# Right-stack tiles at multiples of 128 bytes, and attention's sums over the keys as 512-column products

## The chip, the cores and the metric

The kernel runs on one core of a Trainium2 chip. The metric is the time of one execution on the device in microseconds; three runs of the kernel before gave 663.28 (median), 661.22 and 663.50.

## The reference

One layer of an encoder: a residual stream of 512 positions by 2048 features goes through RMS norm and one input projection, then through two head groups side by side, and one output projection adds it back.

```python
h = rms_norm(x, norm_w)
proj = jnp.einsum('bsd,de->bse', h, w_in)
q, k, v, g_attn, xr, g_lru = jnp.split(proj, SPLITS, axis=-1)
attn_out = attention_group(q, k, v, q_norm_w, k_norm_w)   # 8 heads of 128, 2 key/value heads
lru_out = lru_group(xr, conv_w, conv_b, ...)              # two linear recurrences over 1024 channels
mixed = jnp.concatenate([rms_norm(attn_out, attn_norm_w) * jax.nn.silu(g_attn),
                         rms_norm(lru_out, lru_norm_w) * jax.nn.silu(g_lru)], axis=-1)
return x + jnp.einsum('bse,ed->bsd', mixed, w_out)
```

Attention is full (512 queries by 512 keys, no mask): `s = q k^T * scale`, `p = softmax(s)`, `o = p v`, all in float32. The change concerns the last of the three, the sum over the keys, and where tiles lie in the core's memory (SBUF).

## The kernel before, in words

**Precision.** Each float32 operand of a large product is split into a high and a low part. `mm3` (lines 143 to 147) then makes three products into one accumulator: high x high (line 145), high x low of the moving side (146) and low of the stationary side x high (147). In a row of the profile `mm<-kt,b` the tile named first is the moving operand and the second the stationary one (the weights that are loaded).

**Stages.** The input projection runs in column blocks of 512. First the two blocks of the recurrence's input (`proj_feat`; stationary `wh`/`wl`, moving the turned input `x`), with the recurrence of each half woven into the next block; then keys, values and queries (`proj_tok`; here `x` is stationary and `wh`/`wl` move); then three blocks of gates (`gates`, `proj_feat` again) with attention woven in; a last block of gates; and then the output projection, 672 products on line 890, whose weights `w_out` are combined and split (`oh`, `ol`, lines 704 and 705) as they are needed.

**Attention.** It goes through 8 heads of 4 tiles of 128 queries, step by step (`attention`). In step i: `weights` makes the scores of tile i (3 products of 512 keys, moving `kt`), takes the row maximum on DVE (line 563), the exponential and its sum on ACT (566), the reciprocal on DVE (567), and multiplies by it on POOL (568). `turn_weights` turns tile i-2 with four transposes (575), casts it into the high part on ACT (577) and makes the low part on DVE (578). `values` then sums over the keys for a half head, two tiles: 4 x 3 products with `v` stationary and the turned weights moving, 256 columns wide, whenever the second tile of a half is ready. The sum goes to SBUF by a copy on DVE (590); once per head its square goes through ACT (596) and POOL (597) into a running sum. After each step come two steps of the gate projection, 12 products (`yield STEPS`). DMA issues that prepare sums of `w_out` in memory outside the core are woven into POOL's work (735, 738).

**What sets the order.** On TensorE, and in attention on POOL, the order is that in which the code issues the work (`manual_schedule`); DVE and ACT are ordered by a scheduler in attention and by hand in the output stage. SyncE issues the loads.

**Memory.** Pools are opened on two stacks, left and right, that grow towards each other. The right one starts with a small tile, `end`, of 8 float32 numbers per partition. In the built program every larger tile under it, but for attention's nine `k2`, starts 64 bytes off a multiple of 128; those nine lie under small columns (`sm`, `mx`) and start at a multiple. On the left, the input `x`, the weights `wh`/`wl` of pool `xw`, and the last of the output's operands start at multiples of 128. On the right lie the recurrence's tiles (pool `lru`), `kt`, `v`, the queries and turned weights (`b`, from the ring `b4`), part of the output's operands (pool `fin`, `hq`), and, from the values' split to the end of the query projection, a second pool of `wh`/`wl` named `wx`: `wsplit` (line 196 on) takes the two pools in turn. PSUM, which receives the products, has four buffers for projections (`pj`) and four for the rest (`mm`).

Of the kernel before, what the change touches and what calls it, by code (L numbers as in the profile page):

```python
# [10 lines left out]
F32 = mybir.dt.float32  # L11
F32R = mybir.dt.float32r
AF = mybir.ActivationFunctionType
# [3 lines left out]
P = 128  # L17
SEQ = 512
DM = 2048
KT = DM // P  # L20
NT = SEQ // P
# [9 lines left out]


LRU_K2, LRU_B4 = 12, 9
ATT_K2, ATT_B4 = 9, 9


AHEAD = 600
# [18 lines left out]
def hybrid_kernel(  # L56
# [20 lines left out]
    nc = tc.nc  # L77
# [4 lines left out]
    pools, order = {}, {"left": [], "right": []}  # L82

    def opened(name, side):
        pools[name] = tc.alloc_tile_pool(name=name, bufs=1, side=side, reuse_waits="tile")
        order[side].append(name)
        return pools[name]
# [8 lines left out]
    cp = opened("cp", "left")  # L96
    opened("wr", "left")
    opened("xw", "left")
    opened("end", "right").tile([P, 8], F32, tag="end", name="end")
    hring = opened("hq", "right").ring(8 * 2048, name="hring")  # L100
    aring = pools["hq"].ring(8 * 2048, name="aring")
    opened("lru", "right")
# [5 lines left out]
    def nm(s):  # L108
        cnt[0] += 1
        return f"{s}_{cnt[0]}"  # L110
# [4 lines left out]
    def work():  # L115
        return ("lru", LRU_K2, LRU_B4) if "lru" in pools else ("att", ATT_K2, ATT_B4)

    def k2(dt=F32, shape=(P, SEQ)):
        pool, n, _ = work()
        return pools[pool].tile(list(shape), dt, tag="k2", bufs=n, name=nm("k2"))  # L120

    def b4(dt=F32, shape=(P, 2, SEQ)):
        pool, _, n = work()
        return pools[pool].tile(list(shape), dt, tag="b4", bufs=n, name=nm("b4"))
# [10 lines left out]
    def mm():  # L135
        return ps.tile([P, SEQ], F32, tag="mm", name=nm("mm"))
# [4 lines left out]
    def f(ap):  # L141
        return ap.bitcast(F32)

    def mm3(acc, lh, ll, rh, rl, start, stop):
        nc.tensor.matmul(acc, lh, rh, start=start, stop=False)  # L145
        nc.tensor.matmul(acc, lh, rl, start=False, stop=False)  # L146
        nc.tensor.matmul(acc, ll, rh, start=False, stop=stop)  # L147
# [371 lines left out]
    def turn(rot, h):  # L519

        pt = mm()
        for t in range(NT):
            nc.tensor.transpose(pt[:, t * P : (t + 1) * P], rot[t][:, h, :], ident)  # L523
        return pt

    def split_ps(pt, hi, lo):
        nc.scalar.copy(hi, pt)
        nc.vector.tensor_sub(lo, pt, f(hi))
# [21 lines left out]
    def turned(rot, h):  # L550

        q = b4(F32R)
        split_ps(turn(rot, h), q[:, 0, :], q[:, 1, :])
        return q[:, 0, :], q[:, 1, :]

    def weights(q, g, t):

        qh, ql = q
        tt = slice(t * P, (t + 1) * P)
        sc = mm()  # L560
        mm3(sc, qh[:, tt], ql[:, tt], kth[g], ktl[g], True, True)
        mx = pools["att"].tile([P, 1], F32, tag="mx", bufs=6, name=nm("mx"))
        nc.vector.tensor_reduce(mx, sc, axis=AX.X, op=ALU.max, negate=True)  # L563
        p = k2()
        sm = pools["att"].tile([P, 1], F32, tag="sm", bufs=6, name=nm("sm"))
        nc.scalar.activation(p, sc, AF.Exp, bias=mx, accum_out=sm)
        nc.vector.reciprocal(sm, sm)
        nc.gpsimd.tensor_scalar(p, p, sm, 0.0, op0=ALU.mult, op1=ALU.add)
        return p

    def turn_weights(p, t, pth, ptl):
        tt = slice(t % 2 * P, (t % 2 + 1) * P)
        pt = mm()
        for s in range(NT):
            nc.tensor.transpose(pt[:, s * P : (s + 1) * P], p[:, s * P : (s + 1) * P], ident)  # L575
        p3 = pt.rearrange("p (s q) -> p s q", q=P)
        nc.scalar.copy(pth[:, :, tt], p3)  # L577
        nc.vector.tensor_sub(ptl[:, :, tt], p3, f(pth[:, :, tt]))

    def values(h, half, pth, ptl):  # L580

        gs = slice(h // G * HD, (h // G + 1) * HD)
        o = mm()[:, : 2 * P]
        for s in range(NT):
            mm3(o, vh[s][:, gs], vl[s][:, gs], pth[:, s, :], ptl[:, s, :], s == 0, s == NT - 1)
        if half == 0 and h % 2 == 0:
            ap_[h // 2] = aring.tile([P, 2, SEQ], F32, name=nm("av"))
        av, asum = ap_[h // 2][:, h % 2, :], sums["a"]
        to = slice(half * 2 * P, (half + 1) * 2 * P)
        nc.vector.tensor_copy(av[:, to], o)  # L590
        if half == 1:
            if h == 0:
                nc.scalar.activation(asum, av, AF.Square)
            else:
                sq = k2()
                nc.scalar.activation(sq, av, AF.Square)
                nc.gpsimd.tensor_add(asum, asum, sq)

    def attention(rots):

        qs, ps_, pts = {h: turned(rots[0], h) for h in range(2)}, {}, {}
        yield 13
        last = NH * NT
        for i in range(last + 3):
            h, t = divmod(i, NT)
            if i < last:
                ps_[i] = weights(qs[h], h // G, t)
                if t == 0 and h + 2 < NH:
                    qs[h + 2] = turned(rots[(h + 2) // G], (h + 2) % G)
            j = i - 2  # L610
            if 0 <= j < last:
                h, t = divmod(j, NT)
                if t % 2 == 0:
                    pts[j // 2] = b4(F32R, (P, NT, 2 * P)), b4(F32R, (P, NT, 2 * P))
                turn_weights(ps_.pop(j), t, *pts[j // 2])
            j = i - 3
            if j >= 0 and j % 2 == 1:
                values(j // NT, j // 2 % 2, *pts.pop(j // 2))
            yield STEPS


# [410 lines left out]
    with tc.manual_schedule(engines={mybir.EngineType.Pool}):  # L1032
        weave(fill, attention(rots))
        for _ in range(6):
            next(fill)
# [106 lines left out]
```

## Time and profile before

| | |
|---|---|
| runs | 663.28 us median of 3 (661.22 to 663.50) |
| profiled execution | 663.34 us, of which the span from first to last instruction is 661.5 |
| instructions | 8826 |
| TensorE products | 3067 records |
| attention with the gates | about 280 to 436 us of the span |
| output projection | about 502 to 661 us |

In the rows, PE is TensorE's products, PEld its weight loads, DVE is VectorE, ACT ScalarE, POOL GpSimd, SP SyncE. A product's duration is longer than the distance to the next product's start, since products overlap: a product of 512 columns has a duration of about 390 ns in the rows, and the next starts some 230 ns after it. So distances of starts are read, not durations. "Idle before" is the time in which an engine stood still ahead of a group, with what released it.

### The profile page before, as it was taken

The numbers are of one execution on the slowest core, as the hardware profiler recorded it, in microseconds if no ns is written. First come the engines' busy times: TensorE is split into PE (matmuls) and PEld (weight loads), VectorE is DVE, ScalarE is ACT, GpSimd is POOL, SyncE is SP. The second block draws the span as 40 slices with busy tenths as digits, with TensorE's granted clock in tenths as the row PEclk, the third lists the DMA queues.
The fourth block names the chain that finished last, engine by engine and source line by source line (L and its number), as shares of the span: only waits on it lengthen the run. The fifth ranks groups of instructions, "written<-read, shape, count | busy, mean of one in ns | idle before, by whom it ended". The sixth has DMA issues, their size and how long they took to land.

```text
span 661.5 us, 8826 instructions
## 1 busy us (share of the span) xinstructions
PE 654.1 (99%) x3067; PEld 540.6 (82%) x3067; DVE 490.6 (74%) x851; ACT 346.0 (52%) x639; POOL 91.8 (14%) x121
## 2 busy tenths in 40 slices
PE   8999999999999999999999999999999999999997
PEld 6888888888888888888888888888888878888875
DVE  4879688977687952855865569528967998698994
ACT  3543799489856514454644437435444564333441
POOL 0000000000012301223253335410000000010000
PEclk9999999999999999999999999999999999999999
DMA  8843252322334221345776768762355766585322
GB/s 289 272 143 96 65 141 90 97 64 64 83 106 151 81 90 32 97 138 149 152 168 164 216 128 180 176 153 79 89 164 207 264 215 216 211 290 192 125 83 95
DMA packets 52732, 96.19 MB, mean 145 GB/s; under 512 B 4184, under 2 KB 14544, under 8 KB 52560
## 3 DMA queue, kind: packets, MB, share of 16 engines
q1 hardware_dynamic: 45648, 75.17, 36.0%
q0 software_dynamic: 6720, 19.93, 13.1%
q10 hardware_dynamic: 320, 0.53, 0.3%
q8 instruction: 24, 0.39, 0.2%
q14 instruction: 20, 0.16, 0.1%
HBM read 91.42 MB, written 20.97 MB: 170 GB/s over the span
## 4 chain that ended last, share of the span: by engine, by line
PE 88%; DVE 4%; issue 3%; DMA 3%; POOL 1%; ACT 0%; DVEq 0%; ACTq 0%; POOLq 0%
PE pj L145 19%; PE pj L147 19%; PE pj L146 19%; PE mm L890 9%; PE pj L890 7%; PE mm L146 3%; PE mm L147 3%; PE mm L145 3%; DVE ol L705 2%; PE mm L575 2%; DMA rw<-ts 2%; PE mm L230 1%; PE pj L287 1%; PE mm L523 1%; DMA nw_st<-in_norm_w_dram 1%
## 5 line engine op out<-in xcount | busy, mean ns | idle before, releaser
L145 PE MATMUL pj<-x,wh 128*128 128x512 f32 x376 | 150.2, 400 | 0.0
L147 PE MATMUL pj<-x,wl 128*128 128x512 f32 x376 | 147.1, 391 | 0.0
L146 PE MATMUL pj<-x,wh 128*128 128x512 f32 x376 | 146.7, 390 | 0.0
L204 ACT CAST wh<-wr 128x512 fp32r<-128x512 f32 x144 | 86.5, 617 | 75.9 <-PE pj L147 29.0
L205 DVE TENSOR_TENSOR wl<-wr,wh 128x512 fp32r<-128x512 f32 x144 | 99.5, 711 | 30.7 <-ACT wh L204 30.5
L147 PEld LDWEIGHTS pj<-x,wl 128*128 128x128 f32 x376 | 70.6, 188 | 15.4
L146 PEld LDWEIGHTS pj<-x,wh 128*128 128x128 f32 x376 | 70.8, 188 | 14.0 <-issue 0.5
L145 PEld LDWEIGHTS pj<-x,wh 128*128 128x128 f32 x376 | 70.7, 188 | 13.8 <-issue 0.5
L145 PE MATMUL pj<-wh,x 128*128 128x512 f32 x192 | 75.7, 394 | 0.0
L146 PE MATMUL pj<-wl,x 128*128 128x512 f32 x192 | 75.3, 392 | 0.0
L147 PE MATMUL pj<-wh,x 128*128 128x512 f32 x192 | 75.2, 392 | 0.0
L704 ACT CAST oh<-rw 128x512 fp32r<-128x512 f32 x94 | 54.8, 619 | 31.8 <-PE mm L890 14.5
L705 DVE TENSOR_TENSOR ol<-rw,oh 128x512 fp32r<-128x512 f32 x94 | 60.6, 686 | 9.2 <-ACT oh L704 6.8
L890 PE MATMUL mm<-ol,mh 128*128 128x512 f32 x128 | 50.2, 392 | 0.5 <-DVE ol L705 0.5
L890 PE MATMUL mm<-oh,mh 128*128 128x512 f32 x128 | 50.3, 393 | 0.0
L890 PE MATMUL mm<-oh,ml 128*128 128x512 f32 x128 | 50.2, 392 | 0.0
L577 ACT CAST b<-mm 128x512 fp32r<-128x512 f32 x32 | 18.7, 585 | 58.7 <-PE mm L575 58.7
L563 DVE TENSOR_REDUCE mx<-mm 128x1 f32<-128x512 f32 x32 | 22.0, 688 | 31.2 <-PE mm L147 30.9
L145 PEld LDWEIGHTS pj<-wh,x 128*128 128x128 f32 x192 | 36.1, 188 | 8.1 <-issue 0.2
L146 PEld LDWEIGHTS pj<-wl,x 128*128 128x128 f32 x192 | 36.1, 188 | 8.1 <-issue 0.2
L147 PEld LDWEIGHTS pj<-wh,x 128*128 128x128 f32 x192 | 36.1, 188 | 7.9
L890 PE MATMUL pj<-oh,mh 128*128 128x512 f32 x96 | 37.8, 394 | 0.0
(207 smaller groups left out, 1153.7 us busy)
## 6 DMA issues: line engine op xcount, KB each, us to landing
wr<-in_w_in_dram SPq DMA_DIRECT2D x71, 512.0 KB, 3.7
rw<-in_w_out_dram SPq DMA_DIRECT2D x63, 256.0 KB, 3.9
ts<-in_w_out_dram POOLq DMA_DIRECT2D x24, 512.0 KB, 6.9
rw<-ts SPq DMA_DIRECT2D x31, 256.0 KB, 5.0
ts<-ts POOLq DMA_DIRECT2D x8, 512.0 KB, 5.7
xt<-in_x_dram SPq DMA_DIRECT2D x8, 512.0 KB, 8.2
b<-in_x_dram SPq DMA_DIRECT2D x7, 512.0 KB, 7.7
out_dram<-xt POOLq DMA_DIRECT2D x12, 256.0 KB, 3.0
```

The costliest lines, as they stand in the source:

```text
L145: nc.tensor.matmul(acc, lh, rh, start=start, stop=False)
L146: nc.tensor.matmul(acc, lh, rl, start=False, stop=False)
L147: nc.tensor.matmul(acc, ll, rh, start=False, stop=stop)
L204: nc.scalar.copy(hi, raw[:, k, :])
L205: nc.vector.tensor_sub(lo, raw[:, k, :], f(hi))
L230: nc.tensor.transpose(pt[:, t * P : (t + 1) * P], xc[:, t, ks], ident)
L563: nc.vector.tensor_reduce(mx, sc, axis=AX.X, op=ALU.max, negate=True)
L575: nc.tensor.transpose(pt[:, s * P : (s + 1) * P], p[:, s * P : (s + 1) * P], ident)
L577: nc.scalar.copy(pth[:, :, tt], p3)
L704: nc.scalar.copy(hi, src)
L705: nc.vector.tensor_sub(lo, src, f(hi))
L890: nc.tensor.matmul(bank[name, s], lh[:, a, ts_], rh, start=i == 0 and j == 0, stop=i == 7 and j == 2,)
```

## The change

1. `end` becomes 24 numbers wide (96 bytes instead of 32). In the built program all right-stack tiles then start at a multiple of 128 bytes; attention's `k2` tiles now start 64 off. Nothing else is done to them.
2. The turned weights of a whole head go into one pair of tiles (`pt`, 128 x 4 x 512, high and low), which has two buffers, so one pair. They came from the ring `b4`, a pair per half head; the ring keeps four buffers for the queries.
3. `values` runs once per head: 12 products of 512 columns instead of twice 12 of 256, and one copy of 512 columns.
4. In a step, `values` now stands ahead of `turn_weights`, so that the pair has been read before the next head's first tile is written into it.

```diff
--- before.py
+++ after.py
@@ -31,7 +31,7 @@
 
 
 LRU_K2, LRU_B4 = 12, 9
-ATT_K2, ATT_B4 = 9, 9
+ATT_K2, ATT_B4, ATT_PT = 9, 4, 2
 
 
 AHEAD = 600
@@ -96,7 +96,7 @@
     cp = opened("cp", "left")
     opened("wr", "left")
     opened("xw", "left")
-    opened("end", "right").tile([P, 8], F32, tag="end", name="end")
+    opened("end", "right").tile([P, 24], F32, tag="end", name="end")
     hring = opened("hq", "right").ring(8 * 2048, name="hring")
     aring = pools["hq"].ring(8 * 2048, name="aring")
     opened("lru", "right")
@@ -569,7 +569,7 @@
         return p
 
     def turn_weights(p, t, pth, ptl):
-        tt = slice(t % 2 * P, (t % 2 + 1) * P)
+        tt = slice(t * P, (t + 1) * P)
         pt = mm()
         for s in range(NT):
             nc.tensor.transpose(pt[:, s * P : (s + 1) * P], p[:, s * P : (s + 1) * P], ident)
@@ -577,24 +577,22 @@
         nc.scalar.copy(pth[:, :, tt], p3)
         nc.vector.tensor_sub(ptl[:, :, tt], p3, f(pth[:, :, tt]))
 
-    def values(h, half, pth, ptl):
+    def values(h, pth, ptl):
 
         gs = slice(h // G * HD, (h // G + 1) * HD)
-        o = mm()[:, : 2 * P]
+        o = mm()
         for s in range(NT):
             mm3(o, vh[s][:, gs], vl[s][:, gs], pth[:, s, :], ptl[:, s, :], s == 0, s == NT - 1)
-        if half == 0 and h % 2 == 0:
+        if h % 2 == 0:
             ap_[h // 2] = aring.tile([P, 2, SEQ], F32, name=nm("av"))
         av, asum = ap_[h // 2][:, h % 2, :], sums["a"]
-        to = slice(half * 2 * P, (half + 1) * 2 * P)
-        nc.vector.tensor_copy(av[:, to], o)
-        if half == 1:
-            if h == 0:
-                nc.scalar.activation(asum, av, AF.Square)
-            else:
-                sq = k2()
-                nc.scalar.activation(sq, av, AF.Square)
-                nc.gpsimd.tensor_add(asum, asum, sq)
+        nc.vector.tensor_copy(av, o)
+        if h == 0:
+            nc.scalar.activation(asum, av, AF.Square)
+        else:
+            sq = k2()
+            nc.scalar.activation(sq, av, AF.Square)
+            nc.gpsimd.tensor_add(asum, asum, sq)
 
     def attention(rots):
 
@@ -607,15 +605,18 @@
                 ps_[i] = weights(qs[h], h // G, t)
                 if t == 0 and h + 2 < NH:
                     qs[h + 2] = turned(rots[(h + 2) // G], (h + 2) % G)
+            j = i - 3
+            if j >= 0 and j % NT == NT - 1:
+                values(j // NT, *pts.pop(j // NT))
             j = i - 2
             if 0 <= j < last:
                 h, t = divmod(j, NT)
-                if t % 2 == 0:
-                    pts[j // 2] = b4(F32R, (P, NT, 2 * P)), b4(F32R, (P, NT, 2 * P))
-                turn_weights(ps_.pop(j), t, *pts[j // 2])
-            j = i - 3
-            if j >= 0 and j % 2 == 1:
-                values(j // NT, j // 2 % 2, *pts.pop(j // 2))
+                if t == 0:
+                    pts[h] = [
+                        pools["att"].tile([P, NT, SEQ], F32R, tag="pt", bufs=ATT_PT, name=nm("pt"))
+                        for _ in range(2)
+                    ]
+                turn_weights(ps_.pop(j), t, *pts[h])
             yield STEPS
```

TensorE's order at the first head's sums, before. Here `k` is a tile of softmax weights, `b` a half head's turned weights (high and low), `v` the values, `pj` a gate projection:

```order
L523 MATMUL mm_2802<-ident,ev_2043 128x128
L575 MATMUL mm_2811<-ident,k_551_2721 128x128 x4
L145 MATMUL mm_2818<-b_553_2726,v_1912 128x256
L146 MATMUL mm_2818<-b_554_2727,v_1912 128x256
L147 MATMUL mm_2818<-b_553_2726,v_1912 128x256
```

After nine more such rows the projection goes on. With the change (the end of the scores, the first sums):

```order
L145 MATMUL mm_2871<-kt_2207,b_508_2519 128x512
L146 MATMUL mm_2871<-kt_2207,b_508_2519 128x512
L147 MATMUL mm_2871<-kt_2207,b_508_2519 128x512
L145 MATMUL mm_2882<-pt_2726,v_1912 128x512
L146 MATMUL mm_2882<-pt_2727,v_1912 128x512
L147 MATMUL mm_2882<-pt_2726,v_1912 128x512
```

and behind nine more of these:

```order
L145 MATMUL mm_2882<-pt_2726,v_1921 128x512
L146 MATMUL mm_2882<-pt_2727,v_1921 128x512
L147 MATMUL mm_2882<-pt_2726,v_1921 128x512
L575 MATMUL mm_2900<-ident,k_568_2796 128x128 x4
L145 MATMUL pj_2528<-x_87_440,wh_2855 128x512
```

The sums moved from behind the transposes to between the scores and the transposes, and two steps later, to where the head's fourth tile is there; the transposes are followed by the projection.

DVE at the same place (`mx` maximum, `sm` reciprocal, `av` the copy of the sums; line numbers of the change are one lower at the copy), before:

```order
L578 TENSOR_TENSOR b_573_2810<-mm_2811,b_572_2809 128x4x128
L590 COPY av_2831<-mm_2818 128x256
L563 TENSOR_REDUCE mx_2850<-mm_2846 128x1
L578 TENSOR_TENSOR b_573_2810<-mm_2857,b_572_2809 128x4x128
L205 TENSOR_TENSOR wl_2963<-wr_2960,wh_2962 128x512
```

and with the change:

```order
L578 TENSOR_TENSOR pt_2727<-mm_2840,pt_2726 128x4x128
L205 TENSOR_TENSOR wl_2947<-wr_2944,wh_2946 128x512
L567 RECIPROCAL sm_2836<-sm_2836 128x1
L205 TENSOR_TENSOR wl_2951<-wr_2944,wh_2950 128x512
L563 TENSOR_REDUCE mx_2875<-mm_2871 128x1
L567 RECIPROCAL sm_2878<-sm_2878 128x1
L589 COPY av_2895<-mm_2882 128x512
L578 TENSOR_TENSOR pt_2899<-mm_2900,pt_2898 128x4x128
```

The copy comes once per head, behind the next step's maximum and reciprocal, and the next head's first split stands right behind it. On POOL and SyncE the order is the same as before.

## The prediction

> **What bounds the kernel now.** I read the page first: shares of busy time, then the chain that ended last.
>
> ```profile
> span 661.5 us, 8826 instructions
> PE 654.1 (99%) x3067; PEld 540.6 (82%) x3067; DVE 490.6 (74%) x851; ACT 346.0 (52%) x639; POOL 91.8 (14%) x121
> PEclk9999999999999999999999999999999999999999
> PE 88%; DVE 4%; issue 3%; DMA 3%; POOL 1%; ACT 0%; DVEq 0%; ACTq 0%; POOLq 0%
> ```
>
> TensorE is busy 654.1 of 661.5 us at full clock, and is 88% of the chain. What is left to gain lies inside its stream: the distance from the start of one product to the start of the next, which busy time doesn't show because products overlap. So the second reading is of starts. Where a stretch holds nothing but 512-column products, the first and the last start of one line, with its count, give three products per step (one for each line of `mm3`). Columns: shortest/median/longest duration in ns, first and last start in us.
>
> ```profile
> L147 PE MATMUL pj<-x,wl x67: 388/390/390, 455.1 to 500.0; 128*128 128x512 f32 x67
> L145 PE MATMUL pj<-wh,x x88: 388/390/398, 119.6 to 189.9; 128*128 128x512 f32 x88
> L145 PE MATMUL mm<-k,k x16: 389/390/391, 128.5 to 163.3; 128*128 128x512 f32 x16
> L147 PE MATMUL pj<-wh,x x35: 388/394/398, 202.7 to 226.3; 128*128 128x512 f32 x35
> L147 PE MATMUL pj<-wh,x x28: 389/394/398, 242.4 to 261.2; 128*128 128x512 f32 x28
> ```
>
> Row one: 44.9 us / 66 / 3 = 226.8 ns a product. Rows two and three together (one stretch): 70.3 us / 103 / 3 = 227.5. Row four: 23.6 / 34 / 3 = 231.4. Row five: 18.8 / 27 / 3 = 232.1. The slow stretches are those in which half the weights `wh`, `wl` come from pool `wx`, which lies on the right stack, 64 bytes off a multiple of 128, while `x` lies on the left at a multiple. In row three (`k,k`) both operands lie on the right, 64 off, and the stretch is not slow. So what costs some 5 ns a product goes with operands that differ, in side or in offset; in this kernel the two always go together, and that stays the open question of this forecast.
>
> The third reading is the attention stage, by starts on TensorE:
>
> ```profile
> 295.78 0.60 PE L523 MATMUL mm<-ident,ev 128*128 128x128 f32 x4
> 296.21 0.60 PE L575 MATMUL mm<-ident,k 128*128 128x128 f32 x4
> 296.57 0.37 PE L145 MATMUL mm<-b,v 128*128 128x256 f32 x1
> 296.77 0.28 PE L146 MATMUL mm<-b,v 128*128 128x256 f32 x1
> 296.89 0.28 PE L147 MATMUL mm<-b,v 128*128 128x256 f32 x1
> ...
> 297.96 0.28 PE L147 MATMUL mm<-b,v 128*128 128x256 f32 x1
> 298.08 0.39 PE L145 MATMUL pj<-x,wh 128*128 128x512 f32 x1
> ...
> 300.85 0.39 PE L145 MATMUL mm<-kt,b 128*128 128x512 f32 x1
> ...
> 301.54 0.60 PE L575 MATMUL mm<-ident,k 128*128 128x128 f32 x4
> 301.89 0.48 PE L145 MATMUL pj<-x,wh 128*128 128x512 f32 x1
> 302.21 0.39 PE L146 MATMUL pj<-x,wh 128*128 128x512 f32 x1
> ...
> 304.73 0.39 PE L145 MATMUL mm<-kt,b 128*128 128x512 f32 x1
> ```
>
> A half head's twelve sums take 296.57 to 298.08, 1.51 us: the first 0.20 (it follows transposes), the other eleven 1.31/11 = 119 ns. The twelve projection products behind them take 2.77 us, 230.8 each; the three score products 0.69, 230 each. The first 512-column product behind transposes takes 0.32, some 0.09 more than usual.
>
> **The change, part by part.** The counts, from the groups of this stage (busy, mean ns of one, idle before):
>
> ```profile
> L145 PE MATMUL pj<-x,wh 128*128 128x512 f32 x143 | 57.8, 404 | 0.0
> L145 PE MATMUL mm<-b,v 128*128 128x256 f32 x64 | 19.3, 302 | 0.0
> L147 PE MATMUL mm<-kt,b 128*128 128x512 f32 x32 | 12.6, 394 | 0.0
> ```
>
> *Wider sums.* 192 products of 256 columns in 16 stretches become 96 of 512 in 8. Removed: 16 x 1.51 = 24.2 us (24.1, as the last stretch follows no transposes). Added: 96 x 226.8 ns = 21.8. The stretches now stand ahead of the transposes, so the surcharge that the first sum paid falls on the projection product behind them: 15 x 0.09 = 1.3. Net 24.1 - 21.8 - 1.3 = 1.0 us. At the slow stretches' 232 ns it would be 0.5. Seen the other way: two products of 119 ns against one of 227 save 11 ns, 96 times.
>
> Beside this row stands a rule: the Trainium skill, TensorE: Matmul & The Clock Gate, section Back-to-back issue gap, has the distance of two products as their columns at 2.4 GHz and about 2.5 ns. Halving the number of products would by it save 96 x 2.5 ns = 0.24 us instead of 1.0. The rows show some 13 ns over the columns' time at both widths, so I follow the rows.
>
> *128-byte offsets.* Three stages hold operands that differ today. (a) Lines 145 to 147 with `wx`: 80 steps of three products from 202.7 to 261.2, of which the two rows above show 63; 240 x (231.7 - 226.8) = 1.2 us. (b) Attention: 96 score products (230 against 226.8) 0.3 us; the 429 projection products, both operands on the left already, run at some 230 too, behind sums and transposes. What of that goes away can't be read: nothing, or 429 x 3.2 = 1.4. I take 0.4, because transposes stay in front of them. (c) The output products (line 890):
>
> ```profile
> 116.00:191.00 75.00, 75.00 (x331) 61.99 (x330) 61.09 (x76) 52.24 (x79) 0.00 (x0) 1.00 0.28 79
> 535.00:610.00 75.00, 75.00 (x328) 61.32 (x327) 63.14 (x100) 32.20 (x55) 4.48 (x8) 1.00 0.69 235
> 502.50:530.50 28.00, 28.00 (x124) 22.96 (x123) 26.91 (x43) 16.04 (x26) 0.00 (x0) 1.00 0.73 262
> 610.50:630.00 19.50, 19.50 (x86) 15.87 (x85) 18.19 (x30) 8.34 (x15) 0.86 (x2) 1.00 0.42 138
> ```
>
> (Per stretch: PE, PEld, DVE, ACT, POOL busy with counts, clock, DMA share, GB/s.) In 75 us the output fits three products fewer than the clean stretch: 3 x 227 = 0.7 us, so 1.4 over the 155 us of outputs. But in the last two stretches DVE is busy 26.91 of 28 us and 18.19 of 19.5, and the second ends in a stop:
>
> ```profile
> 630.25 0.39 PE L890 MATMUL mm<-oh,mh 128*128 128x512 f32 x1
> 631.13 0.50 PE L890 MATMUL mm<-ol,mh 128*128 128x512 f32 x1 [0.49 <-DVE ol L705]
> ```
>
> There DVE's splitting of `w_out` (line 705) sets the pace; what TensorE gains there it waits for later. (28 + 19.5)/155 of the 1.4 is 0.4; I keep 1.0.
>
> *What is added at no cost.* Eight copies of 512 columns for sixteen of 256 on DVE, off the chain. The softmax tiles `k2` move the other way, to 64 off; they are the transposes' weights, and today's transposes of `ev` (64 off) and of `k` (0) take the same in the chain of waits:
>
> ```profile
> 295.94 0.44 PE mm L523 x4
> 296.38 0.44 PE mm L575 x4
> ```
>
> The pair of tiles `pt` is single: the next head's first cast waits until the sums have been read. The sums now stand directly ahead of the transposes that this cast needs anyway, so it waits for nothing new; behind it on ACT and DVE stand the next scores' `Exp` and weight splits. The sums themselves come sooner after the fourth tile's split, by one group of transposes:
>
> ```profile
> 302.79 0.69 DVE L578 TENSOR_TENSOR b<-mm,b 128x512 fp32r<-128x512 f32 x1 [0.36 <-ACT b L577]
> ```
>
> Transposes at 301.54, split done at 303.48; sums would start at 301.54 + 0.35 + 2.75 + 0.69 = 305.33, with 1.85 us to spare. Without that cover each head's sums would stall for the difference.
>
> Sum: 1.0 + 1.2 + 0.3 + 0.4 + 1.0 = 3.9 us. The profiled execution took 663.34 us (span 661.5 and 1.8 around it), which is the median of the runs, 663.28. Forecast 663.3 - 3.9 = **659.4 us**.
>
> **Rivals.** *The offset does nothing.* If it is the side of the memory that costs, or the pools' mix, the slow stretches stay. For it: no row here has a left tile 64 off or a right one at 0 in these products. Against: `k,k`, on the right with both operands, is not slow. Then only the wider sums pay: 1.0, 662.3 us. A rule has the same outcome: the Trainium skill, SBUF — State Buffer, Specifications (TRN2), counts 16-byte cachelines, in which a start 64 bytes off is as whole as one at 128, and in Who interferes with whom it gives TensorE independent read ports for moving operand and weights, which would leave nothing for operands to disagree on. That the trace has 231.7 against 226.8 ns isn't explained by either.
>
> *The whole excess goes.* If the projection products in attention run at 226.8 (1.4 instead of 0.4) and DVE keeps up in the output (1.4 instead of 1.0): 663.3 - 5.3 = 658.0 us. For it: stretches without right-stack operands show nothing over 227.5. Against: transposes remain.
>
> *Scaled weights come late: slower.* Between a tile's scores and its transposes two steps later, POOL must have scaled the weights (line 568), between DMA issues that wait. Today the distance holds one stretch of sums (9.5 us); after it a fourth of the tiles, those of one position in each head, have none between: 0.35 + 2.75 + 0.69 + 0.43 + 0.35 + 2.75 + 0.69, less overlaps, about 7.6 us, and the others 9.9 or more. It has been late once:
>
> ```profile
> 395.18 0.39 PE L147 MATMUL mm<-kt,b 128*128 128x512 f32 x1
> ...
> 404.39 0.40 PE L147 MATMUL mm<-kt,b 128*128 128x512 f32 x1
> 404.89 0.66 PE L575 MATMUL mm<-ident,k 128*128 128x128 f32 x4
> ```
>
> ```profile
> 402.55 2.29 POOL L568 TENSOR_SCALAR k<-k,sm 128x512 f32<-128x512 f32 x1
> ```
>
> Scores ended at 395.57, POOL at 404.84: 9.3 us. If that falls on a short distance, the stall is 9.3 - 7.6 = 1.7 us. One eats less than half of the gain; three (5.1) against 3.9 make the kernel slower, and on all eight heads it would be 663.3 - 3.9 + 13.6 = 673 us. With four, 666.2. Against: this tile is at another position in its head, and POOL's order of work is unchanged.
>
> **How the numbers follow.** Forecast's case 0.60, its own range 658.2 to 660.7 (from the sums at 232 ns, 0 or 1.4 in attention, 0 or 0.4 lost in the output); offset does nothing 0.24; whole excess 0.10; late weights 0.06. About 0.5% (3.3 us) is what a measurement of this kernel tells from no change, so "faster" needs less than 660.0. The forecast's case lies below that three times in four: 0.45, and with the third 0.55 faster. The rest of the first, 0.15, and the second, 0.24, are the same; slower takes the last. The range for eight in ten: 657.3 to 662.5, so that it holds the second case at its edge.
>
> **What would show it.** Right: 96 products `mm<-pt,v` of 512 columns, 2.7 us a head; lines 145 to 147 between 202 and 261 us at 227 ns; 75 us of outputs holding 330 or 331 products. Wrong: the 231 to 232 ns there unchanged (second case); an idle time ahead of `L575` released by POOL (last case); a longer stop at 531 or 630 us that ends with DVE's line 705, which would say that DVE took back the output's gain.

## The result, and the profile after

The change takes 661.22 us (median of 15 runs, 660.07 to 662.12), the kernel before 663.21 (15 runs, 661.22 to 664.40): ratio 0.9973, with a 95% interval of 0.9966 to 0.9981. That is a gain of 2.0 us by the medians, 1.3 to 2.3 by the interval, where 3.9 were forecast. It lies within 0.5% of the time before. Left out of the times and ratios below are two executions of one experiment (the moved left stack) that took 1334 and 1697 us, for which its trace shows no reason. The page of the changed kernel opens like the one before:

```profile
span 658.3 us, 8625 instructions
PE 651.0 (99%) x2971; PEld 534.1 (81%) x2971; DVE 488.2 (74%) x843; ACT 345.6 (53%) x639; POOL 92.1 (14%) x121
PE 96%; DVE 1%; DMA 1%; issue 1%; ACT 0%; ACTq 0%; DVEq 0%
```

96 products fewer (2971 records against 3067), full clock, and TensorE is still the chain. The spans of the two traces (661.5 and 658.3 us) differ by more than the medians: the trace of the change is of its shortest execution and reaches the first product with `wh` at 113.0 us instead of 114.9. The traces of all the kernels of the layer reach it between 112.9 and 115.5, with the change as without. So stages are compared, not spans, and the forecast's terms have to be looked for one by one, as distances of starts. In the change, lines behind 590 carry other numbers: the output products are on line 891, `ol` on 706. Everything up to 578 has its number unchanged.

**Attention.** The transposes of the softmax weights (line 575) frame the stage: first and last start of 128. Before, and with the change:

```profile
L575 PE MATMUL mm<-ident,k x128: 270/272/328, 288.0 to 431.5; 128*128 128x128 f32 x128
```

```profile
L575 PE MATMUL mm<-ident,k x128: 270/272/273, 286.0 to 426.6; 128*128 128x128 f32 x128
```

143.5 us against 140.6. Behind the last transposes stood a half head's sums (1.43 us, as no transposes precede them) and now a whole head's; these twelve take 304.73 - 301.99 = 2.74 us in the timeline of TensorE with the change:

```profile
301.99 0.40 PE L145 MATMUL mm<-pt,v 128*128 128x512 f32 x1
302.23 0.39 PE L146 MATMUL mm<-pt,v 128*128 128x512 f32 x1
...
304.50 0.39 PE L147 MATMUL mm<-pt,v 128*128 128x512 f32 x1
304.73 0.60 PE L575 MATMUL mm<-ident,k 128*128 128x128 f32 x4
305.09 0.48 PE L145 MATMUL pj<-x,wh 128*128 128x512 f32 x1
305.40 0.40 PE L146 MATMUL pj<-x,wh 128*128 128x512 f32 x1
```

The stage as a whole went from 143.46 + 1.43 to 140.64 + 2.74 (starts read to 0.01 us): 1.5 us less. The sums alone went from 24.1 to 8 x 2.74 = 21.9. What comes back is seen in the groups by form, at the first product behind the transposes (305.09 to 305.40, 0.31 in place of 0.23):

```profile
L145 PE MATMUL pj<-x,wh 128*128 128x512 f32 x145 | 59.6, 411 | 0.0
L145 PE MATMUL mm<-kt,b 128*128 128x512 f32 x32 | 12.6, 395 | 0.0
```

The mean duration of a gate product (`pj<-x,wh` on line 145) went from 404 to 411 ns: the surcharge moved, as forecast. By the starts, the first product of each of the 33 runs of gate products now has 315 ns to the next one in the mean, where it had 279: 33 x 36 ns = 1.2 us. Net 1.0 of the 1.5. Of the other 0.5, some 0.3 is the stop at 404.4 us, where POOL had been late and which is gone; the rest lies in the score products (`kt,b`, 231 to 229 ns from start to start) and the other gate products (229.9 to 229.4).

**The stretch with pool `wx`, and the output.** Lines 145 and 146 between 242 and 261.5 us, and the output stage in stretches (columns as in the prediction):

```profile
L145 PE MATMUL pj<-wh,x x25: 387/392/396, 242.0 to 258.6; 128*128 128x512 f32 x25
L146 PE MATMUL pj<-wl,x x25: 387/393/398, 242.2 to 258.9; 128*128 128x512 f32 x25
```

```profile
535.00:610.00 75.00, 75.00 (x327) 61.08 (x326) 63.55 (x100) 32.62 (x56) 4.48 (x8) 1.00 0.66 225
```

(16.6 + 16.7)/48/3 = 231.3 ns a product, where the forecast wanted 227; and 327 products in 75 us of outputs, where it wanted 330 or 331 and the kernel before had 328. From the first to the last start the output takes 155.7 us, where it took 155.4. Both stretches that were to gain from the offset gained nothing.

### The profile page after: what moved, and what is told of

Same layout as the page of the kernel before. It is cut to its first block, busy times and chain, and to the rows that moved or that the text cites. A ratio compares the mean times of both kernels' runs of the same rounds, so it can differ in the third digit from the quotient of the medians.

```text
span 658.3 us, 8625 instructions
## 1 busy us (share of the span) xinstructions
PE 651.0 (99%) x2971; PEld 534.1 (81%) x2971; DVE 488.2 (74%) x843; ACT 345.6 (53%) x639; POOL 92.1 (14%) x121
## 4 chain that ended last, share of the span: by engine, by line
PE 96%; DVE 1%; DMA 1%; issue 1%; ACT 0%; ACTq 0%; DVEq 0%
PE pj L145 20%; PE pj L147 20%; PE pj L146 20%; PE mm L891 12%; PE pj L891 9%; PE mm L145 3%; PE mm L147 3%; PE mm L146 3%; PE mm L575 2%; PE mm L230 1%; PE pj L287 1%; PE mm L523 1%; DMA nw_st<-in_norm_w_dram 1%; DVE ol L706 0%; DMA rw<-in_w_out_dram 0%
## 5 line engine op out<-in xcount | busy, mean ns | idle before, releaser
L205 DVE TENSOR_TENSOR wl<-wr,wh 128x512 fp32r<-128x512 f32 x144 | 98.0, 701 | 30.3 <-ACT wh L204 30.3
L577 ACT CAST pt<-mm 128x512 fp32r<-128x512 f32 x32 | 18.8, 586 | 53.1 <-PE mm L575 53.1
L891 PE MATMUL pj<-ol,mh 128*128 128x512 f32 x96 | 37.9, 394 | 0.0
```

What stands on the lines that cost most here:

```text
L205: nc.vector.tensor_sub(lo, raw[:, k, :], f(hi))
L891: nc.tensor.matmul(bank[name, s], lh[:, a, ts_], rh, start=i == 0 and j == 0, stop=i == 7 and j == 2,)
```

## The experiments

Each timed kernel ran beside the kernel before on the same chip; ratios are to that. Addresses below are those in the built programs.

**The two parts of the change apart.** First the offset alone, on the kernel before:

```diff
-    opened("end", "right").tile([P, 8], F32, tag="end", name="end")
+    opened("end", "right").tile([P, 24], F32, tag="end", name="end")
```

> The kernel before with the end tile widened to 96 bytes and nothing else: all right-stack tiles but attention's k2 go to multiples of 128 bytes. My forecast (the offset makes operands that differ slow) expects about 2.6 us less than before, 660.6 us, with lines 145 to 147 between 202 and 261 us at 227 ns a product. The rival (the side of the memory costs, not the offset) expects no change, within 0.4 us of before, and 231 to 232 ns there. From the changed kernel's profile, where that stretch still has 231.5 ns, I now hold the rival likelier.

662.65 us, ratio 0.9999 (0.9990 to 1.0007): nothing. Then the change with `end` at its old size:

```diff
-    opened("end", "right").tile([P, 24], F32, tag="end", name="end")
+    opened("end", "right").tile([P, 8], F32, tag="end", name="end")
```

> The change without the wider end tile: 512-column sums in one pair of tiles, right-stack tiles 64 bytes off as before. If the sums alone carry the gain: 1.0 us for 96 products less and up to 0.5 for the late softmax tile that POOL caused before, so 661.7 to 662.3 us and the same as the change within 0.5 us. If the offset carries part of it: the change is 1 us or more faster than this.

661.11 us, ratio 0.9978 (0.9969 to 0.9988). The wider sums are the whole gain of the change as far as these intervals tell; 128-byte starts bring nothing that shows.

**The second pool of weights away.** With the change, all of `wh`, `wl` come from the left pool, which has half as many buffers:

```diff
-        opened("wx", "right")
```

> The change without the second weight pool wx on the right stack, so that lines 145 to 147 read both operands from the left all the time. If products whose two operands lie on opposite sides are slow: the stretch from 202 to 261 us falls from 231.5 to 227 ns a product, 240 x 4.5 = 1.1 us less than the change, unless the splits, which then have four buffers instead of eight, come late. If something else in that stretch is slow (the query projection itself, the moving weights): 231 ns remain and the time is that of the change.

660.66 us, ratio 0.9967 (0.9957 to 0.9978), 0.45 below the kernel with the sums alone on the same chip, with intervals that overlap; 1.1 below the change was expected. The slow stretch is gone:

```profile
L145 PE MATMUL pj<-wh,x x27: 389/389/389, 241.7 to 259.4; 128*128 128x512 f32 x27
```

17.7/26/3 = 226.9 ns, and from the first to the last product with `wh` the trace has 144.9 us, where the change has 146.1: the 1.1 is there, in the stage, though the medians show less. So it is the pair of a right-stack and a left-stack operand that costs, and the change left that cost in place. Whether it is the side or the address was still open.

**Products alone.** Three kernels leave out the layer and run streams of 36 products on TensorE, from tiles that all start at the same address modulo 512. The first varies the tile (near, far, either end of the memory) and then pushes one or both operands on by some bytes. The number in `sw` (weights) and `mv` (moving operand) is the offset in bytes; here is a stream of the second kernel, cut out:

```python
for i in range(36):
    nc.tensor.matmul(a, sw("n", 0, i), mv("b", 128, i), start=i == 0, stop=i == 35)
```

> Not the layer: TensorE alone, 54 streams of 36 products of 512 columns, each stream on a line of its own, with moving operand and weights at chosen places in sixteen tiles of 12.5 KiB from the bottom (a) to the top (p), all constant ones; most of the output is not written. First 30 streams: moving operand in b, weights in each other tile, then moving in o. Last 24: four pairs (b with o, o with b, b with c, o with n) with the moving operand 64, 32 or 96 bytes off, the weights 64 or 32 off, or both 64. If the side costs: 227 ns where both are low or both high, 231 to 235 where not, with an edge between tiles h (ends at 103552) and j (starts at 116352). If the offset costs: 227 everywhere in the first 30 and more in the last 24. If neither: 227 throughout, and the cost comes from what else runs in the kernel.

Of the thirty streams without an offset, over all places, 29 have the same 226.7 ns from start to start, and the first of all, which begins with some 430 ns a product, comes down to the same: the side does not matter. With an offset, three streams of one pair of tiles in the timeline (start, time to the last one's end): moving operand 64 bytes on, weights 64 on, both 64 on:

```profile
300.65 8.41 PE L160 MATMUL mm<-to,tb 128*128 128x512 f32 x36
308.90 8.56 PE L163 MATMUL mm<-to,tb 128*128 128x512 f32 x36
317.30 8.34 PE L166 MATMUL mm<-to,tb 128*128 128x512 f32 x36
```

Less the last one's 0.39 us, over 35 distances: 229.1, 233.4 and 227.1 ns. Both operands 64 off are as good as none. What costs is the *difference* of their addresses, and to within 0.3 ns the same in all four pairs of tiles that were tried.

The change's "multiple of 128" then had to be read again. Its right-stack tiles lie 384 bytes beyond a multiple of 512 and the left ones at a multiple: still apart. A second kernel of streams looked for the modulus:

> Streams of 36 products on TensorE alone, the layer itself is left out; every tile starts at the same address modulo 512 bytes, one line of the program per stream. Theory now: a product of 512 columns costs 226.7 ns from start to start when its moving operand and the weights have the same address modulo 512 bytes, and 229 to 233 ns otherwise. It expects 226.7 for a moving operand pushed on by 0 and by 512 bytes; 228.9 at 64; and 231 to 233 at 128, 192, 256, 320, 384 and 448. If the modulus is smaller, 256 (and with it 128 or 384) is back at 226.7. Rival: what counts is only the offset modulo 128 bytes, as the change assumed: 226.7 at 128, 256, 384 and 512. Two further streams for each of 64, 128 and 32 bytes alternate the offset from product to product: in the first, each moving operand matches its own weights and not the next product's; in the second the next product's and not its own. If the cost comes from the next weights' load beside the running product, the first is slow and the second fast; if from the product's own pair, the reverse. Products of 256 columns: 119 at equal offsets; the surcharge of 2 to 7 ns per product at others, if it is one per load of weights, or half of it, if it goes by columns.

Moving operand on by 64, 128, 192, 256, 320, 384, 448 and 512 bytes, in that order:

```profile
35.16 8.42 PE L56 MATMUL mm<-tb,tn 128*128 128x512 f32 x36
43.41 8.53 PE L59 MATMUL mm<-tb,tn 128*128 128x512 f32 x36
51.78 8.57 PE L62 MATMUL mm<-tb,tn 128*128 128x512 f32 x36
60.19 8.37 PE L65 MATMUL mm<-tb,tn 128*128 128x512 f32 x36
68.39 8.42 PE L68 MATMUL mm<-tb,tn 128*128 128x512 f32 x36
76.65 8.53 PE L71 MATMUL mm<-tb,tn 128*128 128x512 f32 x36
85.01 8.57 PE L74 MATMUL mm<-tb,tn 128*128 128x512 f32 x36
93.42 8.36 PE L77 MATMUL mm<-tb,tn 128*128 128x512 f32 x36
```

The second four repeat the first: the modulus is 256, not the 512 that was expected, and not the change's 128. A stream can need ten products to settle (the one at 256: 229, 229, 233, 236, 224, 231, 236, 228, 233, 231, then 226 to 227 for good), so means of the last 27 distances are the better figures:

```
difference modulo 256, bytes      0      64     128    192
streams, ns                     227.0   228.9  232.4  233.4
output products in the layer    226.8   230.3  232.7  233.3
```

The second row is from the layer itself: mean distances of neighbouring products of the output stage without a stop, grouped by their operands' addresses (0: 667 of them with 480 bytes at `end`, below; 64 and 192: 240 and 106 in the kernel with the sums alone; 128: 346 in the change). Streams and layer differ by 1.4 ns at 64 and by 0.3 at most elsewhere; a further stream at 128, in the third kernel below, has 233.5. Products of 256 columns are indifferent: 120.0 ns at equal addresses, 117.8 at 64 apart and 118.5 at 128. So the sums of 256 columns, 128 apart before, should have lost nothing by it.

Two streams each for 64, 128 and 32 bytes alternated the offset so that a moving operand matched its own weights or the next product's. All six ran between 228.2 and 231.7 ns, neither kind at 227: whether the pair itself or the next weights' load disturbs the running product isn't told by them. The layer shows the same. Between 202 and 261 us products with weights from the two pools alternate by threes: in the change those with equal addresses have 232.3 ns to the next start, those 128 apart 231.1. In its output, the 321 products with equal addresses have 228.2, with unequal ones among them. An equal pair among unequal ones is not as fast as in a stream of equal ones.

The Trainium skill, SBUF — State Buffer, Who interferes with whom, gives TensorE one read port for the moving operand and an independent one for the weights. The streams do not bear that out in time: up to 7 ns of a product (1.9 at 64 bytes, 6.4 at 192) hang on how the two addresses stand to each other, with no other engine at work.

**The layer with the operands' addresses equal.** 480 bytes at `end` bring the right stack to the left one's address modulo 512, and two columns with 8 buffers in place of 6 bring keys and queries to one address:

```diff
-    opened("end", "right").tile([P, 24], F32, tag="end", name="end")
+    opened("end", "right").tile([P, 120], F32, tag="end", name="end")
-        mx = pools["att"].tile([P, 1], F32, tag="mx", bufs=6, name=nm("mx"))
+        mx = pools["att"].tile([P, 1], F32, tag="mx", bufs=8, name=nm("mx"))
-        sm = pools["att"].tile([P, 1], F32, tag="sm", bufs=6, name=nm("sm"))
+        sm = pools["att"].tile([P, 1], F32, tag="sm", bufs=8, name=nm("sm"))
```

> The change with 480 bytes in place of 96 at the end of the right stack, and the two small columns of attention (the row maxima and sums) with 8 buffers each in place of 6, so that every product in three parts finds its two operands at the same address modulo 512 bytes; the instructions and their order on every engine stay the change's. Theory (equal residues modulo 512): the mean distance of products from 202 to 261 us falls from 231.5 to about 227 ns (about 1.1 us), that of the output's products from 230.5 to about 227 (up to 1.9 us, part of which a later wait for VectorE may take back), and attention's scores give 0.3 to 0.5: 657.5 to 659.3 us, 2 to 3.5 below the change. Rival (the residue is without effect in the layer, as the change's own offset was): 661.1, as the change.

657.77 us, ratio 0.9926 (0.9912 to 0.9940): 3.4 us below the change by the medians, and with a lower time than both kernels. The two stretches, and the waits of TensorE (us in total, times, longest):

```profile
L145 PE MATMUL pj<-wh,x x24: 389/389/389, 241.6 to 257.3; 128*128 128x512 f32 x24
L146 PE MATMUL pj<-wl,x x24: 389/389/389, 241.9 to 257.5; 128*128 128x512 f32 x24
```

```profile
535.00:610.00 75.00, 75.00 (x332) 62.10 (x331) 63.87 (x101) 33.08 (x57) 4.47 (x8) 1.00 0.67 225
```

```profile
PE mm L891 <- DVE ol L706: 0.8, 1, 0.8
PE pj L891 <- DVE ol L706: 0.4, 1, 0.4
```

(15.7 + 15.6)/46/3 = 226.8 ns, and 332 products in 75 us. Over 155 us of outputs, 5/327 is 2.4 us. DVE took back part: TensorE waits 1.2 us for line 706, where the waits of the change have

```profile
PE mm L891 <- DVE ol L706: 0.5, 1, 0.5
```

From the first to the last start the output takes 153.9 us, 1.8 less than with the change. The scores come down from 229.1 to 226.7 ns, but attention gains nothing by it: the frame of line 575 is 140.8 us, and the gate products in it take 0.5 us more.

The offset by itself, 480 bytes on the kernel before:

```diff
-    opened("end", "right").tile([P, 8], F32, tag="end", name="end")
+    opened("end", "right").tile([P, 120], F32, tag="end", name="end")
```

> The kernel before with 480 bytes in place of 32 at the end of the right stack and nothing else; attention's sums stay 256 columns wide. Theory (equal residues modulo 512): 1.1 us from 202 to 261 and 1 to 1.9 in the output, 2 to 3 us below before: 660.2 to 661.2 us. Rival (an offset does nothing, as with 96 bytes): 663.0.

659.38 us, ratio 0.9952 (0.9937 to 0.9966). With 96 bytes there was no gain, with 480 there is one of 3.2 us (2.3 to 4.2): more than the sums bring.

With 224 bytes in place of 480 (and the 8 buffers), the right stack lies 256 off, modulo 512:

```diff
-    opened("end", "right").tile([P, 120], F32, tag="end", name="end")
+    opened("end", "right").tile([P, 56], F32, tag="end", name="end")
```

> As with 480 bytes at the right stack's end and 8 buffers for the two small columns, but with 224 bytes: right-stack tiles are then 256 bytes off the left ones modulo 512. Theory (modulus 256, as in the streams): as with 480 bytes, 657 to 658.5 us. Rival (512 in the layer): the scores' pairs alone are right, 660.6 us.

658.01 us, ratio 0.9932 (0.9920 to 0.9944), as with 480: 256 is the modulus in the layer too.

Last, the other stack. The change as it is, with 128 unused bytes ahead of the left stack's tiles:

```diff
-    ident = const([P, P], "ident")
+    _, ident = const([P, 32], "pad"), const([P, P], "ident")
```

> The change as it stands, with one unused constant of 128 bytes put ahead of the left stack's tiles: the right stack stays where the change put it, and the left one moves by 128 bytes. The 132 products with weights of pool wx and the output's 348 products with one operand on each stack now have equal addresses modulo 256 bytes; the 96 score products, both of whose operands lie on the right, stay 128 apart. Theory (only the two operands' difference modulo 256 counts): the distances from 202 to 261 us and in the output fall to 227 ns, 480 products x (232.4 - 226.7) = 2.7 us less than the change, 658 to 659 us. Rival (each operand has an address of its own that suits it, and the right stack's 480-byte end happened to meet it): no gain, 661 us, or a loss since the left stack's own pairs have left theirs.

Ratio 0.9947 (0.9933 to 0.9962), from executions of 658.1 to 660.7 us. In the output:

```profile
535.00:610.00 75.00, 75.00 (x333) 62.10 (x332) 63.83 (x101) 32.68 (x56) 4.47 (x8) 1.00 0.70 234
```

The change's right stack, left where it is, is fast with a left stack that has moved. In these products no operand has an address of its own that suits it; the difference decides. About 1 us of what was expected is missing, and it is missing in attention:

```profile
L575 PE MATMUL mm<-ident,k x128: 271/272/273, 287.3 to 429.0; 128*128 128x128 f32 x128
```

```profile
L145 PE MATMUL mm<-kt,b 128*128 128x512 f32 x32 | 12.9, 404 | 0.0
```

141.7 us against 140.6. The score products last 404 ns in the mean against 395, and they hold what is missing: from start to start they take 236.6 ns, against 229.1 in the change and 226.7 with 480 bytes. With the steps into and out of them that is 1.0 us more than with 480 bytes, while the gate products take the same 89.1 us in both. The scores' two operands lie at the very addresses that they have in the change, 128 apart; what has moved is `x` and `wh` of the gate products ahead of them. So the operands' own difference is not the whole condition for three products between others: with 480 bytes on the kernel before they are 128 apart again and take 236.7 ns, and in the kernel before 231.1. Why the same difference has three prices there stays open.

**Why attention stays above 227.** In all these kernels attention's gate products run at 229 to 231 ns (the first behind transposes left out), though both operands' addresses are equal. A third kernel of streams put four float32 transposes ahead of 12 or 3 products:

> TensorE alone, the layer itself is left out. First streams of 36 products whose moving operand is pushed on by 0, 16, 32, 48, 64, 96, 128, 160, 224 and 240 bytes against the weights: 226.7 ns at 0 and between 228 and 234 at all others, if only equal addresses are fast. Then six times four float32 transposes followed by 12 or by 3 products, of 512 and of 256 columns, and six times the transposes alone. The forecast moved the cost of the first product behind transposes from a 256-column product (81 ns more than its neighbours) to a 512-column one (90 ns more). If this cost belongs to the transposes and not to the product, a block with 12 and one with 3 products of 512 columns differ by 9 x 226.7 = 2040 ns and one with 256 by 9 x 119 = 1070 ns, and the time beyond products and transposes is the same 80 to 90 ns at both widths; if a wider product hides part of it, the wider one's is smaller.

```profile
112.84 0.60 PE L90 MATMUL mm<-idn,kf 128*128 128x128 f32 x4
113.19 3.02 PE L93 MATMUL mm<-tb,tn 128*128 128x512 f32 x12
116.05 0.60 PE L90 MATMUL mm<-idn,kf 128*128 128x128 f32 x4
...
130.00 0.60 PE L97 MATMUL mm<-idn,kf 128*128 128x128 f32 x4
130.35 0.94 PE L100 MATMUL mm<-tb,tn 128*128 128x512 f32 x3
131.13 0.60 PE L97 MATMUL mm<-idn,kf 128*128 128x128 f32 x4
...
151.64 2.78 PE L118 MATMUL mm<-idn,kf 128*128 128x128 f32 x24
```

Four transposes by themselves take 0.44 us (24 start 109 ns apart). A block with three products repeats every 1.13 us, which is 0.44 + 3 x 0.227 and 0.01 more: the first product's surcharge is only the transposes' own time, since that product starts 0.35 us after the first of them, not 0.44. It moves with the transposes and costs nothing beside them, at either width. A block with twelve repeats every 3.2 us: the nine further products take 2.07, 230 ns each. Behind an interruption a stream of 512-column products settles only from its eighth to eleventh distance on; one of 256 columns is at 117 to 120 ns from its second (blocks of 1.87 and 0.80 us: 119 ns for each further one). Of the offsets added in this kernel, 16, 32, 48, 96, 160 and 224 bytes cost 231.6 to 234.4 ns; 240 did not (226.7, in one stream), against the expectation that only equal addresses are fast.

Two kernels varied the address of the identity matrix, the transposes' other operand, on the kernel with 224 bytes and 8 buffers, so with all products' pairs equal. 128 bytes ahead of it and behind it make transposes equal too:

```diff
-    ident = const([P, P], "ident")
+    _, ident, _ = (const([P, n], t) for n, t in ((32, "p1"), (P, "ident"), (32, "p2")))
```

> The kernel with 224 bytes at the right stack's end and 8 buffers for the two small columns, and 128 unused bytes ahead of and behind the identity matrix: the transposes too (identity against softmax weights and queries) now have equal addresses modulo 256 bytes; they were 128 apart. Left open so far: attention's projection products run at 229 ns although both their operands are equal, and at 231 where the left stack was moved. Theory A (the transposes' own difference disturbs what follows): attention's mean comes down from 229.1 towards 227, 550 products x 2 ns = 1.1 us, 656.9 us. Theory B (any transposes upset the rhythm of the next eight or so products, as in the streams, whatever their addresses): 229 stays, 658.0 us.

and 192 and 64 bytes (`48` and `16` in place of the two `32`) leave them 64 apart:

> As the kernel before this one (all products' operands at equal addresses modulo 256 bytes), but with 192 bytes ahead of the identity matrix and 64 behind it, so that the transposes' two operands are 64 bytes apart instead of equal; nothing else moves. Question left open: with the left stack moved, and with 480 bytes alone, the transposes happened to be 64 apart, and attention's projection products then ran at 231 ns against 228 to 229 where they were 0, 128 or 192 apart. Theory A (64 bytes between the transposes' operands shift the rhythm of what follows): 231 here too, attention 1.1 to 1.4 us longer, 659.3 us. Theory B (the transposes' addresses don't matter, the 231 came from the scores' or the values' pairs there): 228.4 to 229, 658.0 us.

658.35 us, ratio 0.9927 (0.9914 to 0.9941), and 657.90, ratio 0.9923 (0.9910 to 0.9937), as without them (658.01). Line 575's frame is 140.4 and 140.8 us, 0.4 of the latter in a single stop; without the moved matrix it is 140.8. That is theory B of both: the transposes' addresses are worth 0.3 us at most. That their presence keeps the gate products at 230 ns is what the streams show; no kernel of the layer was run without transposes.

## Why the prediction was right or wrong, by its steps

The time, 661.2, lies inside the range of 657.3 to 662.5, but nearer the second case than the forecast: about half of the gain came, and it is the wider sums' part. It is inside because the range was drawn to hold the second case, not because the terms held.

**What bounds the kernel** was read rightly: TensorE, at full clock, and the distance of starts as what can still be gained. The finding that the slow stretches have one operand on each stack was right too, and it was right to name side and offset as not told apart. But neither of the two was the cause.

**Wider sums**, 1.0: right. 24.1 to 21.9 us, less the moved surcharge of 1.2: 1.0 by the starts; the kernel with the sums alone gained 1.5 (0.8 to 2.1), the lost stop of 0.3 included. The rule that halving the number of products saves only 2.5 ns each (the Trainium skill, TensorE: Matmul & The Clock Gate, Back-to-back issue gap) was rightly passed over: in the streams, two products of 118.5 to 120 ns against one of 227 save 10 to 13.

**128-byte offsets**, (a) 1.2 and (c) 1.0, and the score products' 0.3 in (b): these are the step that failed. Operands do cost by their addresses, but by the difference of the two modulo 256, and the change leaves right and left 128 apart. By the table above it moved 132 products with `wx` from 192 to 128 (0.1 us gained), 240 output products from 64 to 128 (0.6 lost) and 108 from 192 to 128 (0.1 gained); the scores were 128 apart before and after. That is a loss of 0.4 where 2.5 of gain stood; in the traces the output became 0.3 us longer and the stretch with `wx` stayed at 231.7 ns (231.9 before). The step took "one at a multiple of 128, the other 64 off" for the cause, and equality modulo 128 for equality. Its rows held a pair that speaks against that, and it put it among the operands that differ: the score products, at 230 ns, have both operands on the right and both 64 off. They are 128 apart in the built program. With the addresses really equal, (a) is 1.1 us and the output gains 1.7 of 2.4, the rest going into the wait for DVE's line 706 that the step on the output had foreseen. The scores then run at 226.7 ns, but the frame of attention gets no shorter. The term for the projections in attention (0.4 in (b)) had no cause: both operands were equal all along, and they run at 230 as the streams' twelve products behind transposes do.

**Added at no cost**: right. No new wait for `pt` or for DVE's copies appeared; TensorE's waits in attention are none.

**The rivals.** "The offset does nothing" came out nearest: it gave 662.3, the sums alone, and measured were 661.22. Its reason, that the side costs, fell: the streams from all over the memory are alike. The rule beside it, that a start 64 bytes off is as good as one at 128, holds for two operands that are both 64 off, and not for one. "Late weights" did not occur; the one stop of that kind that the kernel before had at 404 us is gone, which is 0.3 us that no term held.

## What to carry to other kernels

When a float32 product that runs back to back is a few ns slower in one stage than in another, compare the addresses of its moving operand and its weights modulo 256 bytes. Where they differ, a pad at the bottom of one pool that makes them equal costs a few hundred bytes a partition, and here it gave more than a change of the algorithm's tiling did. And a correlation that most of a kernel's rows show in one form only ("64 off") should be held against the rows that don't fit, here the scores, and be priced as a rival with a real chance until a small stream of products has separated its parts.

## What the runs showed that was not expected

- In streams, the difference of the two operands' addresses modulo 256 bytes sets the distance of 512-column products: 227 ns at 0, 228.9 at 64, 231 to 234 at the others that were tried, except 226.7 at 240.
- Products of 256 columns do not care, 117.8 to 120.0 ns.
- Behind an interruption (other products, transposes) a stream of 512-column products with equal addresses can take seven to ten products, of 224 to 236 ns, until it settles at 227.
- Short runs do not go by their own pair alone: the three score products, 128 apart each time, take 229, 231 or 237 ns, depending on where the other tiles lie.
